# Two encoder layers on one core: the state-space tables' preparation on a new schedule, and the first q and k products begun on 256 tokens

## The chip, the core and the metric

The kernel runs on one NeuronCore of a Trainium2 chip. The time is the device time of one execution in microseconds (us). A core has TensorE (PE, with its weight loads shown as PEld), VectorE (DVE), ScalarE (ACT), GpSimd (POOL), and SyncE (SP), which here only issues DMAs. Each engine takes its own instructions strictly in the order in which they were written for it; a semaphore makes an instruction wait for another engine or for a DMA.

## The reference

Two layers over 1024 tokens of width 1024, each with a token mixer and a SwiGLU, both between RMSNorms. The first mixer is forgetting attention with 16 heads of 64, the second a state-space mixer (S5) with 64 groups of 16 channels and 64 states.

```python
for i in range(DEPTH):
    h = rmsnorm(x, mix_pre_gain[i])
    m = fox_mixer(h, ...) if i % 2 == 0 else s5_mixer(h, ...)
    x = x + rmsnorm(m, mix_post_gain[i])
    h = rmsnorm(x, ffn_pre_gain[i])
    x = x + rmsnorm((silu(h @ w_gate) * (h @ w_up)) @ w_down, ffn_post_gain[i])

# fox_mixer
proj = h @ w_in                       # q, k, v, gate, forget logits
q, k = rmsnorm(heads(q), q_gain), rmsnorm(heads(k), k_gain)
c = cumsum(log_sigmoid(f_logit + b_f))
s = q @ k.T * scale + c[q] - c[k]     # causal
o = softmax(s) @ v * sigmoid(gate);  return o @ w_out

# s5_mixer: x[t] = A x[t-1] + Bbar u[t];  y = Re(C x) + d * u
a = exp(lam * dt);  Bbar = (a - 1) / lam * B      # depends on the parameters alone
```

All of it is float32; a product is made of three float32r matmuls on high and low parts (high by high, high by low, low by high).

## The kernel before

**Order.** The code is written as generators that hand over to each other. A list scheduler then writes each engine's queue: it takes the instructions in the order of the code (some with a raised or lowered priority) and puts each where its own estimate of durations says that it is ready. On the chip the queues are followed as written, however long things really take.

**Start.** The 1024 tokens are eight blocks of 128. For each block `first_norm` squares the rows on ACT (L302), scales them on DVE (L325) or POOL (L318, L323), transposes them on PE in eight matmuls (L333) and splits the result into a high part (`hT`, cast on ACT, L335) and a low part (subtracted on DVE, L336). In the kernel before, four blocks are finished (`run(first_norm(range(0, 4), ...))`) and then the other four are woven with `qkv`, whose first work is the projection of q and of k for the first 512 tokens: 24 matmuls of 128x512 each, q's at L283, k's at L272 to L274. Their weights come as two DMAs of 512 KB (`raw`), are split on POOL (L253, L254), and are asked for behind the fourth and the sixth block of x. Behind that follow the forget logits (L392, L393) and q and k of tokens 512 to 1023 (L272 again).

**Gate and up of layer 0.** `gate_up` makes the gate and up products for 11 pairs of 128-column slices by a Strassen-like scheme: a pair is 14 steps of 12 matmuls of 128x512 (L853), each step into one of the bank pairs X, Y, Z of PSUM. X alternates between two bank pairs from one pair of slices to the next; Y is banks 4 and 5, Z banks 6 and 7. ACT and DVE split weights (L822, L823) and take results out of PSUM (L891 to L915).

**The tables.** Into these steps goes the preparation of the state-space tables, the generator `s5_params`: 27 pieces, one for each `next(beside, None)`, and a function `when(p, s)` says behind which step s of which pair p one is called. Pieces 1 to 8 are small DVE work (`s5_small`, L1028 to L1184), 9 and 10 transpose the C matrices (L1207, loaded by L1201), and pieces 11 to 27 make, for each of eight chunks of channels, two things in turn:

- odd piece: `finish` of the chunk before, which is eight transposes (L1223), one ACT copy into a page named `s5w1` (L1225) and its DMA to DRAM (`T_d`, L1226); then eight POOL operations (L1237, L1238, four L1241) that make `cp`. Their scratch `kg` is in the same page `s5w1`, so that they wait until that DMA has landed. ACT copies `bs` beside it (L1240).
- even piece: eight small products `pk` on PE (L1255) that read `cp`, their copies on ACT (L1258), and six POOL operations that make `bp` (L1298 to L1300), which the next odd piece transposes.

In the kernel before, the pieces stand at steps 8, 10, 12 of pair 0, at 5, 6, 8, 10, 12 of pair 1, at 5, 8, 12 of pair 2 and at 5 and 12 of every later pair. Their PSUM (`T.S`) is the bank pair Y (`T.slots = (4,)`).

The kernel's later stages (down projection, S5, the second layer's products) are not touched.

Of the kernel before, what the change touches and what calls it, by code (L numbers as in the profile page):

```python
# [10 lines left out]
F32R = mybir.dt.float32r  # L11
# [24 lines left out]
def f32(ap):  # L36
    return ap.bitcast(F32)
# [100 lines left out]
def weave(*streams):  # L138

    st = [[g, 0.0, max(t, 1e-6)] for g, t in streams]  # L140
    while st:
        s = min(st, key=lambda e: e[1] / e[2])
        try:
            s[1] += next(s[0])
        except StopIteration:
            st.remove(s)


def run(g):
    for _ in g:  # L150
        pass


def chain(*gs):
    for g in gs:
        yield from g


class Trunk:
# [113 lines left out]
        mm(ps, lh, rl, start=False, stop=False)  # L273
        mm(ps, ll, rh, start=False, stop=stop)  # L274

    def fm(self, ps, w, hT, half, step=4, apart=False):

        wh, wl = w
        h, l = hT[half]
        if apart:  # L280
            for n, (a, b) in enumerate(((wh, h), (wl, h), (wh, l))):
                for k in range(8):
                    self.nc.tensor.matmul(ps, a[:, k, :], b[:, k, :], start=n == k == 0, stop=n == 2 and k == 7)  # L283
                yield 0.65 * 8 / 3
            return
        for k in range(8):
            self.mm3(ps, wh[:, k, :], wl[:, k, :], h[:, k, :], l[:, k, :], k == 0, k == 7)
            if k % step == step - 1:
                yield 0.65 * step
# [118 lines left out]
        nc.vector.tensor_tensor_scan(z, ones, t1, 0.0, op0=ALU.mult, op1=ALU.add)  # L408
        nc.sync.dma_start(self.csum, z)

    def qk_proj(self, w, hT, hf, st, apart=False):
        nc = self.nc
        if "p" not in st:
            st["p"] = [self.R(f"p{i}", dt=F32R) for i in st["pages"]]
        ps = self.pb(self.proj)
        yield from self.fm(ps, w, hT, hf, apart=apart)
        X, Y = st[hf] = self.R("pt", (P, 2, 512)), self.R("pt", (P, 2, 512), F32R)
        with self.tc.high_priority(AHEAD):
            nc.scalar.copy(X[:, 1], ps)
            nc.vector.tensor_mul(X[:, 0], X[:, 1], X[:, 1])  # L420
        nc.scalar.copy(Y[:, 0], X[:, 0])
        nc.vector.tensor_sub(Y[:, 1], X[:, 0], f32(Y[:, 0]))
# [51 lines left out]
        tr(1)  # L474
        yield 0.5

    def qkv(self, hT, res, hp):


        v = []  # L480
        a, f, b = self.qkp if hp else ([9, 11, 8], [7, 35, 10], [12, 13, 14])
        q, k = dict(pages=a + f[2:]), dict(pages=f[:2])
        self.qkp = a[:2] + f[:1], b, [a[2], f[2], f[1]]
        if hp == 0:
            self.lsub, self.hcopy = self.nc.gpsimd, self.nc.gpsimd.tensor_copy
            wq, wk = self.take(), self.take(0)
            self.lsub, self.hcopy = self.nc.vector, self.nc.scalar.copy
            yield from self.qk_proj(wq, hT, 0, q, True)
            yield from self.qk_proj(wk, hT, 0, k)
            yield from self.forget_logits(hT)  # L490
            yield from self.qk_proj(wq, hT, 1, q)
            self.proj = (0, 1, 2, 3)
            with self.tc.issue_after(self.sqrt.ins):
                self.nc.scalar.preload_act_table_set(LNEXP)
            self.forget_sum()
            yield from self.qk_norm(0, 0, q)
            yield from self.qk_proj(wk, hT, 1, k)
            wv = self.take()
            yield from self.qk_norm(1, 0, k)
            yield from self.qk_norm(0, 1, q)  # L500
        else:
            wk = self.take()
            yield from self.qk_proj(wk, hT, 0, k)
            yield from self.qk_proj(wk, hT, 1, k)
            wq = self.take()
            yield from self.qk_norm(1, 0, k)
            yield from self.qk_proj(wq, hT, 0, q)
            yield from self.qk_norm(1, 1, k)
            yield from self.qk_proj(wq, hT, 1, q)
            wv = self.take()  # L510
            yield from self.qk_norm(0, 0, q)
        last = self.qk_norm(0, 1, q) if hp else self.qk_norm(1, 1, k)
        yield from self.v_proj(wv, hT, v, last)
        res.update(q=q["p"], k=k["p"], v=v)
# [132 lines left out]
    def fox(self, hT, og_d, begin, outr):  # L647
        c = [{} for _ in range(8)]
        o = [None] * 8
        weave((self.qkv(hT, c[0], 0), 11.0), (begin, 4.0))  # L650
        self.proj = PROJ
        self.R.set(pt=list(range(25, 29)))
        att = self.attend(c, o)
        held = [next(att)]

        def until(hp):
            while held and held[0][1] <= hp:
                yield held[0][0]
                held.clear()
                for x in att:  # L660
                    held.append(x)
                    break

        for hp in range(8):
            if hp == 7:
                a, f, b = self.qkp
                pages = f + [15, 16, 29, 33] + a + b + [17, 18, 19]
                self.R.set(woh=pages[0::2], wol=pages[1::2], **outr)
            fill = [self.pre_out(4)] if hp == 7 else [self.qkv(hT, c[hp + 1], hp + 1)]
            if hp:  # L670
                fill.insert(GP, self.gate(hp - 1, o, hT, og_d))
            weave((until(hp), 28.5 * AX), (chain(*fill), 34.0 * (hp < 7) + 10.4 * (hp > 0)))
        run(self.gate(7, o, hT, og_d))
# [125 lines left out]
    def gate_up(self, B, g_d, beside=iter(()), when=lambda p, s: False):  # L799
# [7 lines left out]
        nc, R = self.nc, self.R  # L807
        V = nc.vector
        n = NF // 2
# [64 lines left out]
        for p, s in order:  # L874
# [23 lines left out]
            a, b, x = steps[s // 2]  # L898
# [53 lines left out]
            if p == 0 and s > 11:  # L952
                prep[s - 10](1)
            if when(p, s):
                next(beside, None)
        yield

# [602 lines left out]
def trunk(ctx: ExitStack, tc: tile.TileContext, A, out):  # L1560
    T = Trunk(ctx, tc, A, out)
    nc, R = T.nc, T.R
    rg = lambda a, b: list(range(a, b))
    Wi = A["fox_w_in"][0]
    og_d = T.dram("og_d", [D, D])
# [31 lines left out]
    g_d = [[T.dram(f"g{i}{x}_d", [NF // 2, P, D if x < 3 else 512]) for x in range(4)] for i in range(2)]  # L1597
    T.ffn_plan(0, g_d[0], [T.rows(A["s5_w_in"][0], k * P, T.s5_w_in_cut(k)) for k in range(8)])
    for f in range(8):
        T.plan(T.cols(A["s5_w_glu"][0], f * P)[:3] + (("glu",) * 2 if f == 0 else (None,) * 2))  # L1600
        if f >= 1:
# [7 lines left out]
    OUT0 = dict(x=[23, 24], y=[25, 26, 27],  # L1609
                gn=[21, 22], ogk=[32])  # L1610
# [9 lines left out]
    hT = T.new_hT()  # L1620
    g0 = []

    def first_norm(tbs, banks):
        for tb in tbs:
            pool = tb in (5, 7)
            T.norm(xs[tb], g0[0] if pool else gps, ys[tb], pool, R("j") if pool else None)
            T.to_fm(ys[tb], T.hT_dst(hT, tb), banks)
            yield 1.0
# [10 lines left out]
    for tb in range(8):  # L1639
        xs[tb], ys[tb] = R("x"), R("y")  # L1640
        nc.sync.dma_start(xs[tb], x0[tb * P:tb * P + P, :])
        if tb == 3:
            T._load(0)
        if tb == 5:
            T._load(1)
            g0.append(T.gain("gn", A["mix_pre_gain"][0]))
    T.fox_setup()
    run(first_norm(range(0, 4), (0, 1, 2, 3)))
    T.fox(hT, og_d, first_norm(range(4, 8), (2, 3)), OUT0)
    xr = x0.rearrange("(p b) d -> p b d", b=8)  # L1650
    R.set(hold=[28, 30, 31, 34, 36, 37], t1=[20], ah=[3, 4, 20], al=[5, 6, 21], er=[29, 32])
    first = {0: (8, 10, 12), 1: (5, 6, 8, 10, 12), 2: (5, 8, 12)}
    B = Operands(T)
    gu = T.gate_up(B, g_d[0], T.s5_params(), lambda p, s: s in first.get(p, (5, 12)))
    end = T.out_proj(lambda tb: xr[:, tb, :], A["mix_post_gain"][0], A["ffn_pre_gain"][0], x1_d, turns, B, lambda: next(gu))
    orr = out[0].rearrange("(p b) d -> p b d", b=8)
    gp = []
# [12 lines left out]
        ys[tb] = m, T.rstd(m, R("fj"), out=T.rr5[:, tb:tb + 1])  # L1670

    R.set(ops=rg(7, 14) + [19] + rg(15, 19), a2=[36, 37], S=[23, 24], s=[26, 27, 25], up=[22, 35], gr=[7, 8], t1=[32], ez=[33], **EARLY)
    T.slots = (4,)
    gu.send(end)
    T.slots = (0, 2)
    R.set(t=[15, 16], gh=[9, 37, 3], gl=[10, 36, 18], wdh=[11, 12, 35, 28], wdl=[13, 5, 29, 32], m=rg(19, 27), s=[27], rx=[4], ry=[33, 34])
# [23 lines left out]
    B = Operands(T)  # L1700
    gu = T.gate_up(B, g_d[1])
# [60 lines left out]
```

## Time and profile before

| what | value |
|---|---|
| median of three runs (lowest, highest) | 2391.63 us (2391.47, 2392.79) |
| the profiled execution | 2391.49 us, of it 2389.4 us from first to last instruction |
| PE busy | 2342.8 us, 98% of the span |
| DVE, ACT, POOL busy | 1688.9, 1198.0, 446.8 us |
| PE on the chain that ended last | 80% of the span |
| mean granted TensorE clock | 0.997 |

"Busy" of PE counts a matmul from its start to its modelled end, and matmuls overlap; the pace of PE is therefore read from start to start. A row of the timeline gives start, duration, engine, line, operation, output and inputs, count, and in brackets the idle time before it and what ended it. A row of a table of windows gives, for each engine, busy time and number of instructions, then the granted clock, the share of the DMA engines and GB/s. Of the groups of `raw` and `g_d` transfers each moves 512 KB or 256 KB; the median from issue to landing is 4.3 us for a 512 KB weight load of gate.

### The profile page before, as it was taken

To read this page: it belongs to the slowest core of one execution; us is meant where nothing else is said; L and a number is where in the kernel's file an instruction comes from. 1 tells how busy PE (TensorE), PEld (TensorE's weight loads), DVE (VectorE), ACT (ScalarE), POOL (GpSimd) and SP (SyncE) were. 2 spreads that over 40 slices of the span, in tenths; PEclk is the share of its full clock that TensorE was granted. 3 is DMA by queue.
4 is the path that set the end of the run, shared out by engine and by line. 5 is a ranking of instruction groups with operands and counts; after the bars stand their busy time and mean duration, and the time that the engine had idled before them with its cause. 6 is when DMAs were issued, how large, how long until landed. Compare 5 with 4: busy or idle time off the path is not lost.

```text
span 2389.4 us, 31474 instructions
## 1 busy us (share of the span) xinstructions
PE 2342.8 (98%) x11687; PEld 1942.2 (81%) x11687; DVE 1688.9 (71%) x2687; ACT 1198.0 (50%) x2029; POOL 446.8 (19%) x425
## 2 busy tenths in 40 slices
PE   8999999999999999999999999999999999999997
PEld 6788888888788878888888889888888888888886
DVE  6867777678678966667768686853795655655867
ACT  6766676677745334434554662332463333333444
POOL 3222221223300034545620002410000000000003
PEclk9999999999999999999999999999999999999999
DMA  5121112211333444343598753543434323238874
GB/s 158 39 63 50 58 49 67 63 45 62 127 129 111 120 116 138 118 138 118 185 323 315 267 172 98 153 134 106 132 93 142 110 93 119 92 111 277 283 233 158
DMA packets 256587, 320.33 MB, mean 134 GB/s; under 512 B 34289, under 2 KB 184097, under 8 KB 256434
## 3 DMA queue, kind: packets, MB, share of 16 engines
q1 hardware_dynamic: 256434, 318.33, 41.6%
q8 instruction: 91, 1.49, 0.3%
q14 instruction: 62, 0.51, 0.1%
HBM read 240.56 MB, written 77.72 MB: 133 GB/s over the span
## 4 chain that ended last, share of the span: by engine, by line
PE 80%; DVE 10%; ACT 4%; issue 3%; DMA 1%; POOL 1%; SPq 0%; DVEq 0%; ACTq 0%; POOLq 0%
PE ps L853 32%; PE ps L974 16%; PE ps L272 7%; PE ps L273 7%; PE ps L274 7%; PE ps L615 2%; PE ps L596 2%; PE ps L558 1%; DVE ps L562 1%; PE ps L559 1%; DVE y L325 1%; ACT y L302 1%; DVE ptl L600 1%; POOL o L622 1%; PE ps L101 1%
## 5 line engine op out<-in xcount | busy, mean ns | idle before, releaser
L853 PE MATMUL ps<-B,ah 128*128 128x512 f32 x992 | 306.7, 390 | 0.8 <-DVE B L90 0.6
L974 PE MATMUL ps<-wdh,gl 128*128 128x512 f32 x616 | 240.1, 390 | 1.9 <-DVE gl L254 1.9
L974 PE MATMUL ps<-wdh,gh 128*128 128x512 f32 x616 | 240.6, 391 | 0.7 <-DVE s L895 0.6
L974 PE MATMUL ps<-wdl,gh 128*128 128x512 f32 x616 | 240.3, 390 | 0.8 <-DVE wdl L254 0.8
L853 PE MATMUL ps<-ops,ah 128*128 128x512 f32 x704 | 219.7, 393 | 2.1 <-ACT s L910 2.1
L853 PEld LDWEIGHTS ps<-B,ah 128*128 128x128 f32 x992 | 186.2, 188 | 40.7 <-DVE B L90 1.2
L272 PE MATMUL ps<-hT,wh 128*128 128x512 f32 x504 | 200.8, 398 | 1.1 <-DVE pt L436 0.6
L274 PE MATMUL ps<-hT,wl 128*128 128x512 f32 x504 | 198.5, 394 | 0.0
L273 PE MATMUL ps<-hT,wh 128*128 128x512 f32 x504 | 197.6, 392 | 0.0
L853 PE MATMUL ps<-B,al 128*128 128x512 f32 x496 | 193.2, 390 | 0.0
L253 ACT CAST gh<-gr 128x1024 fp32r<-128x1024 f32 (+1 forms) x78 | 81.1, 1039 | 163.3 <-PE ps L974 127.5
L853 PEld LDWEIGHTS ps<-ops,ah 128*128 128x128 f32 x704 | 132.2, 189 | 31.4 <-ACT s L910 2.6
L254 DVE TENSOR_TENSOR gl<-gr,gh 128x1024 fp32r<-128x1024 f32 (+1 forms) x78 | 98.0, 1258 | 79.7 <-ACT gh L253 79.5
L1713 POOL TENSOR_TENSOR y<-m,s 128x512 f32<-128x512 f32 x4 | 6.5, 1625 | 759.0 <-DMA raw<-in_ffn_w_down_dram 750.1
L823 DVE TENSOR_TENSOR al<-raw,ah 128x1024 fp32r<-128x1024 f32 x84 | 110.8, 1321 | 46.7 <-ACT ah L822 46.3
L553 POOL TENSOR_TENSOR An<-An,cmask 128x128 f32<-128x128 f32 x128 | 78.7, 616 | 341.7 <-DVE mx L562 309.9
L600 DVE TENSOR_TENSOR ptl<-ps,pth 128x512 fp32r<-128x512 f32 x192 | 102.4, 551 | 56.6 <-ACT pth L599 56.2
L853 PE MATMUL ps<-ops,al 128*128 128x512 f32 x352 | 137.8, 392 | 0.0
L974 PEld LDWEIGHTS ps<-wdh,gl 128*128 128x128 f32 x616 | 115.7, 188 | 26.8 <-DVE gl L254 2.7
L974 PEld LDWEIGHTS ps<-wdh,gh 128*128 128x128 f32 x616 | 115.7, 188 | 26.1 <-DVE s L895 1.3
L974 PEld LDWEIGHTS ps<-wdl,gh 128*128 128x128 f32 x616 | 115.7, 188 | 24.9 <-DVE wdl L254 1.5
L822 ACT CAST ah<-raw 128x1024 fp32r<-128x1024 f32 x84 | 88.3, 1052 | 90.3 <-PE ps L853 81.5
(379 smaller groups left out, 5913.4 us busy)
## 6 DMA issues: line engine op xcount, KB each, us to landing
raw<-in_ffn_w_down_dram SPq DMA_DIRECT2D x98, 512.0 KB, 5.2
gr<-g_d SPq DMA_DIRECT2D x76, 512.0 KB, 4.5
raw<-in_ffn_w_gate_dram SPq DMA_DIRECT2D x44, 512.0 KB, 4.3
raw<-in_ffn_w_up_dram SPq DMA_DIRECT2D x44, 512.0 KB, 4.2
g_d<-s SPq DMA_DIRECT2D x66, 256.0 KB, 2.2
raw<-in_fox_w_in_dram SPq DMA_DIRECT2D x32, 512.0 KB, 4.3
g_d<-up SPq DMA_DIRECT2D x44, 256.0 KB, 3.2
g_d<-up SPq DMA_DIRECT2D x21, 512.0 KB, 3.0
```

The source lines that it names most:

```text
L253: self.hcopy(h, src)
L254: self.lsub.tensor_sub(l, src, f32(h))
L272: mm(ps, lh, rh, start=start, stop=False)
L273: mm(ps, lh, rl, start=False, stop=False)
L274: mm(ps, ll, rh, start=False, stop=stop)
L553: nc.gpsimd.tensor_add(An[h][:, qs], An[h][:, qs], self.cmask)
L596: nc.tensor.transpose(p2[:, i], p[:, (g + i) * P:(g + i + 1) * P], self.ident)
L600: nc.vector.tensor_sub(dl, p2[:, 0:n], f32(dh))
L822: nc.scalar.copy(h, src)
L823: V.tensor_sub(l, src, f32(h))
L853: nc.tensor.matmul(bank, x[:, k], y, start=start and k == i == 0, stop=True, skip_group_check=True)
L974: nc.tensor.matmul(bank, x[:, j, t], y[:, j], start=start and i == 0, stop=True, skip_group_check=True)
```

## The change

Three edits.

1. Two blocks of 128 tokens are normalised instead of four before `qkv` begins, and `qk_first` makes q and k of tokens 0 to 511 in pieces of 256 tokens (`quarter`): q's and k's first 256 tokens, with one `next(begin)` (a further block) behind each, then the second 256 of both. The weight loads move up behind the second and the fourth block of x. The transposes go to PSUM banks 6, 7, 2 and 3 in turn.
2. The table's pieces get a list of steps for every pair. There are still 27. With the list, odd and even pieces of one chunk stand five steps apart in two chunks, six in four and eight in one; before they stood seven apart in all.
3. Their PSUM is the X bank pair that the running pair does not use.

```diff
+    def quarter(self, ps, w, hT, c):
+        wh, wl = w
+        h, l = hT[0]
+        s = slice(256 * c, 256 * c + 256)
+        for n, (a, b) in enumerate(((wh, h), (wl, h), (wh, l))):
+            for k in range(8):
+                self.nc.tensor.matmul(ps[:, s], a[:, k, :], b[:, k, s], start=n == k == 0, stop=n == 2 and k == 7)
+            yield 0.9
+
+    def qk_first(self, ws, hT, sts, begin):
...
+        for p, w in zip(ps, ws):
+            run(self.quarter(p, w, hT, 0))
+            next(begin)
+        for p, w, st in zip(ps, ws, sts):
+            yield from self.quarter(p, w, hT, 1)
+            self.qk_out(p, 0, st)
...
-            yield from self.qk_proj(wq, hT, 0, q, True)
-            yield from self.qk_proj(wk, hT, 0, k)
+            yield from self.qk_first((wq, wk), hT, (q, k), begin)
...
-        weave((self.qkv(hT, c[0], 0), 11.0), (begin, 4.0))
+        weave((self.qkv(hT, c[0], 0, begin), 9.0), (begin, 4.0))
...
             if when(p, s):
+                self.slots = (p % 2 * 2 ^ 2 ^ self.X0,)
                 next(beside, None)
...
+        if tb == 1:
+            T._load(0)
         if tb == 3:
-            T._load(0)
+            T._load(1)
         if tb == 5:
-            T._load(1)
...
-    run(first_norm(range(0, 4), (0, 1, 2, 3)))
-    T.fox(hT, og_d, first_norm(range(4, 8), (2, 3)), OUT0)
+    run(first_norm(range(0, 2), (2, 3, -2, -1)))
+    T.fox(hT, og_d, first_norm(range(2, 8), (2, 3, -2, -1)), OUT0)
...
-    first = {0: (8, 10, 12), 1: (5, 6, 8, 10, 12), 2: (5, 8, 12)}
+    table = {0: (9, 12), 1: (6, 9, 12), 2: (4, 8, 12), 3: (2, 5, 9), 4: (2, 7, 12), 5: (5, 11), 6: (3, 9), 7: (2, 7, 12),
+             8: (4, 10), 9: (2, 8), 10: (2, 8)}
...
-    gu = T.gate_up(B, g_d[0], T.s5_params(), lambda p, s: s in first.get(p, (5, 12)))
+    gu = T.gate_up(B, g_d[0], T.s5_params(), lambda p, s: s in table[p])
...
-    T.slots = (4,)
```

What this does to the queues is shown at three places. First PE at the start of the program, before: `y` are the normalised blocks that are transposed, `hT` their high and low parts, `wh` and `wl` the split weights of q.

```order
L333 MATMUL ps<-ident,y_110 128x128 x8
L333 MATMUL ps<-ident,y_113 128x128 x8
L333 MATMUL ps<-ident,y_116 128x128 x8
L333 MATMUL ps<-ident,y_119 128x128 x8
L283 MATMUL ps<-hT_99,wh_269 128x512 x8
```

The same place after (the transposes are now L327, and the products of 256 tokens L412):

```order
L327 MATMUL ps<-ident,y_110 128x128 x8
L327 MATMUL ps<-ident,y_113 128x128 x8
L412 MATMUL ps<-hT_99,wh_221 128x256 x8
L412 MATMUL ps<-hT_99,wl_222 128x256 x8
L412 MATMUL ps<-hT_100,wh_221 128x256 x8
L412 MATMUL ps<-hT_99,wh_227 128x256 x5
L327 MATMUL ps<-ident,y_118 128x128 x8
L412 MATMUL ps<-hT_99,wh_227 128x256 x3
```

The products of q and of k now stand behind the second block, and the third block's transposes behind 29 of them.

Next ACT in the second half of pair 2 (no. 2), before: `s_7713` and `up_7714` are the pair's results out of PSUM, `R` the page that holds `bs`, `bb` a result of the small DVE work.

```order
L908 COPY s_7713<-ps 128x512
L1240 COPY R_775_7414<-bb_7612 64x4x16 x2
L908 COPY up_7714<-ps 128x512
L1240 COPY R_775_7414<-bb_7612 64x4x16 x2
L822 CAST ah_7773<-raw_7479 128x1024
L910 COPY s_7713<-ps 128x512
```

The same place after:

```order
L926 COPY s_7707<-ps 128x512
L926 COPY up_7708<-ps 128x512
L840 CAST ah_7775<-raw_7478 128x1024
L928 COPY s_7707<-ps 128x512
L840 CAST ah_7799<-raw_7725 128x1024
L928 COPY up_7708<-ps 128x512
L1259 COPY R_782_7533<-bb_7910 64x4x16 x4
```

The copies of `bb` moved from between the results of steps 4, 5 and 6 to behind that of step 7.

Last ACT between the copy of an odd piece's transposes (`s5w<-ps 128x1024`) and the copies of the even piece behind it (`s5w<-ps 16x4x128`), before; the rows between are weight splits and results of the steps, and `S` and `raw` are weights.

```order
L1225 COPY s5w_847_8196<-ps 128x1024
L822 CAST a_867_8391<-raw_8097 128x512
L903 COPY s_8233<-ps 128x512
L903 COPY up_8234<-ps 128x512
L822 CAST ah_8278<-S_8275 128x1024
L891 ACTIVATE s_8233<-s_8233 128x512
L822 CAST ah_8298<-raw_8021 128x1024
L908 COPY s_8302<-ps 128x512
L908 COPY up_8303<-ps 128x512
L1240 COPY R_775_7414<-bb_7612 64x4x16
L1258 COPY s5w_862_8346<-ps 16x4x128 x2
```

The same chunk after (the pieces stand at steps 7 and 12 of pair 4):

```order
L1244 COPY s5w_866_8409<-ps 128x1024
L909 ACTIVATE s_8323<-s_8323 128x512
L840 CAST ah_8470<-raw_8393 128x1024
L909 ACTIVATE s_8232<-s_8232 128x512
L840 CAST ah_8496<-S_8493 128x1024
L909 ACTIVATE s_8323<-ps 128x512
L840 CAST a_886_8637<-raw_8343 128x512
L1277 COPY s5w_874_8522<-ps 16x4x128 x2
```

Eight rows of the steps' work and a copy of `bs` stood between the two, now six rows. On PE, 84 matmuls of 128x512 stood between the transposes and the `pk` products of every chunk; now 60, 72, 72, 60, 72, 72 and 96 for the chunks 1 to 7, counted in the two queues.

More of the change, by code (lines that the diff above doesn't have):

```diff
@@ L274, in mm3, with fm @@
         mm(ps, ll, rh, start=False, stop=stop)
-    def fm(self, ps, w, hT, half, step=4, apart=False):
+    def fm(self, ps, w, hT, half, step=4):
         wh, wl = w
         h, l = hT[half]
[L280 to L285, printed above, removed]
         for k in range(8):
@@ L409, in forget_sum, with qk_proj @@
         nc.sync.dma_start(self.csum, z)
-    def qk_proj(self, w, hT, hf, st, apart=False):
-        nc = self.nc
+    def quarter(self, ps, w, hT, c):
[7 more added lines that the diff above has]
+    def qk_first(self, ws, hT, sts, begin):
+        for st in sts:
+            st["p"] = [self.R(f"p{i}", dt=F32R) for i in st["pages"]]
+        ps = [self.pb(self.proj) for _ in ws]
+        for p, w in zip(ps, ws):
[4 more added lines that the diff above has]
+            self.qk_out(p, 0, st)
+    def qk_proj(self, w, hT, hf, st):
         if "p" not in st:
@@ L415, in qk_proj, with qk_out @@
         ps = self.pb(self.proj)
-        yield from self.fm(ps, w, hT, hf, apart=apart)
+        yield from self.fm(ps, w, hT, hf)
+        self.qk_out(ps, hf, st)
+    def qk_out(self, ps, hf, st):
+        nc = self.nc
         X, Y = st[hf] = self.R("pt", (P, 2, 512)), self.R("pt", (P, 2, 512), F32R)
@@ L475, in v_proj, with qkv @@
         yield 0.5
-    def qkv(self, hT, res, hp):
+    def qkv(self, hT, res, hp, begin=None):
         v = []
```

## The prediction

> **What bounds the kernel.** I read the page's shares first, then windows, then PE's waits, and last the timelines of all engines where PE waits.
>
> ```profile
> PE 2342.8 (98%) x11687; PEld 1942.2 (81%) x11687; DVE 1688.9 (71%) x2687; ACT 1198.0 (50%) x2029; POOL 446.8 (19%) x425
> 760.00:900.00 140.00, 135.01 (x603) 110.34 (x602) 114.58 (x236) 53.48 (x86) 21.27 (x16) 0.98 0.42 114
> 900.00:1100.00 200.00, 200.00 (x957) 164.36 (x956) 137.85 (x148) 80.83 (x125) 106.52 (x80) 1.00 0.40 127
> 859.04 5.60 PE L853 MATMUL ps<-ops,a 128*128 128x512 f32 x24
> 864.48 0.62 PE L853 MATMUL ps<-B,ah 128*128 128x512 f32 x2
> ```
>
> PE is busy 98% of the span. In gate and up it loses 5 us between 760 and 900 and nothing from 900 to 1100, so every wait that the change takes from PE or gives to PE counts in full. The pace is (864.48 - 859.04) / 24 = 0.2267 us for a 128x512 matmul; a step of 12 is 2.72 us.
>
> **Part 1, the start.**
>
> ```profile
> 8.74 3.89 PE L333 MATMUL ps<-ident,y 128*128 128x128 f32 x16 [2.65 <-DVE rr L309]
> 15.83 3.78 PE L333 MATMUL ps<-ident,y 128*128 128x128 f32 x16 [3.19 <-DVE y L325]
> 19.48 2.31 PE L283 MATMUL ps<-hT,wh 128*128 128x512 f32 x8
> 29.84 1.03 PE L333 MATMUL ps<-ident,y 128*128 128x128 f32 x8
> 30.64 0.48 PE L272 MATMUL ps<-hT,wh 128*128 128x512 f32 x1
> 34.25 1.87 PE L393 MATMUL ps<-hT,wf 128*48 128x512 f32 x7
> 41.71 0.39 PE L272 MATMUL ps<-hT,wh 128*128 128x512 f32 x1
> 12.44 1.06 ACT L335 CAST hT<-ps 128x512 fp32r<-128x512 f32 x2
> 8.11 1.06 ACT L302 ACTIVATE y<-x 128x1024 f32<-128x1024 f32 x1 [0.28 <-DMA x<-in_x_dram]
> 11.22 1.04 POOL L253 CAST wh<-raw 128x1024 fp32r<-128x1024 f32 x1 [8.55 <-DMA raw<-in_fox_w_in_dram]
> 79.64 0.28 PE L558 MATMUL ps<-p,p 128*128 128x256 f32 x1
> 79.88 0.40 PE L274 MATMUL ps<-hT,wl 128*128 128x512 f32 x1
> ```
>
> Now PE waits 3.19 us for block 2, and q's first product starts at 19.48; the first product of q's second 512 tokens starts at 41.71. With the change q needs only the casts of block 1, the first of which ends at about 13.0. Its weights come third in the queue, where the third block of x landed at 8.1 (ACT squares it then); with POOL's 1.04 us cast they are there long before. The third block lands one transfer later, hidden, because ACT now squares it behind the casts of block 0. From 13.0 PE has: 96 products of 256 tokens at 0.12 (two of that width take 79.64 to 79.88) = 11.5; six blocks of transposes at 0.80 (29.84 to 30.64) = 4.8; the forget logits, 34.25 to 41.71, = 7.5; one product of the q norm, 0.2. That is 24.0, and 37.0 without losses. Losses: at the start the clock is half (16 transposes take 3.78 us at 15.83, eight take 0.80 later). I take it as half until about 16.6, one stretch of PE work of the length that ran slow before: 3.6 us at half rate loses 1.8. The products behind the transposes of blocks 3 and 7 wait for a cast each, 0.7 in all. So 39.5 against 41.71: -2.2 us. If the clock rises at once, -4.0; if only at 19.98 as late as before, -0.5. The PSUM banks and the earlier weight loads I cost at nothing; the covers are the waits named.
>
> **Part 2, the waits of pair 2.**
>
> ```profile
> 831.92 0.50 PE L853 MATMUL ps<-T,al 128*128 128x512 f32 x1 [1.36 <-DVE al L823]
> 842.06 0.82 PE L853 MATMUL ps<-ops,ah 128*128 128x512 f32 x2 [2.14 <-ACT s L910]
> 844.80 1.94 PE L1207 MATMUL ps<-ident,s5w 128*128 128x128 f32 x8 [1.49 <-DMA s5w<-in_s_c_re_dram]
> 839.96 0.49 ACT L1240 COPY R<-bb 64x64 f32<-64x64 f32 x2 [2.08 <-DVE bb L1184]
> 829.78 0.95 DVE L1153 TENSOR_SCALAR s5t<-R 128x448 f32<-128x448 f32 x1
> 842.60:849.40 6.80, 5.31 (x17) 4.05 (x16) 3.94 (x5) 2.44 (x4) 0.00 (x0) 0.50 0.98 183
> 849.40:856.20 6.80, 6.80 (x35) 5.67 (x35) 3.19 (x4) 1.79 (x3) 4.39 (x4) 1.00 0.02 5
> ```
>
> These are the 5 us: 1.36 for a weight split that stands in DVE's queue behind the small table work, 2.14 because ACT stands at a copy of `bb` that DVE has not made, 1.49 for the C matrices, whose load waited for the same DVE work. After them the granted clock is 0.50 for 6.8 us; the 5.31 us of PE work there take twice their time, 2.65 lost. Together 7.64.
>
> The list puts pieces 4 to 8 later (step 9 of pair 1 to step 12 of pair 2, before step 5 to 12 of pair 1) and the copies of `bb` behind step 7's result. So the 2.14 should go, the 1.49 too (the C transposes now come four steps, 10.9 us, behind their loads), and the clock stays up. The DVE work itself is only moved: I leave one wait like the 1.36, with bounds 0 and 3.5 (1.36 + 2.14). Part 2: -7.64 + 1.4 = -6.2.
>
> **Part 3, the chunks.** An odd piece's transposes start a chain that an even piece's products wait for.
>
> ```profile
> 901.05 1.03 PE L1223 MATMUL ps<-ident,s5w 128*128 128x128 f32 x8
> 917.38 3.33 POOL L1241 TENSOR_TENSOR s5w<-s5w 64x512 f32<-64x512 f32 x2
> 921.07 1.05 PE L1255 MATMUL ps<-s5w,R 128*16 128x128 f32 x16
> 1021.59 1.03 PE L1223 MATMUL ps<-ident,s5w 128*128 128x128 f32 x8
> 1022.85 1.03 ACT L1225 COPY s5w<-ps 128x1024 f32<-128x1024 f32 x1
> 1023.92 0.38 SPq L1226 DMA_DIRECT2D T_d<-s5w  x1
> 1027.68 1.10 POOL L1237 TENSOR_TENSOR s5w<-cc,pw 128x512 f32<-128x512 f32 x1 [12.18 <-DMA T_d<-s5w]
> 1035.22 3.85 POOL L1241 TENSOR_TENSOR s5w<-s5w 64x512 f32<-64x512 f32 x2
> 1041.61 0.62 PE L1255 MATMUL ps<-s5w,R 128*16 128x128 f32 x8
> 1052.01 3.43 POOL L1300 TENSOR_TENSOR s5w<-s5w,s5w 128x512 f32<-128x512 f32 x2
> 1061.77 1.03 PE L1223 MATMUL ps<-ident,s5w 128*128 128x128 f32 x8
> 1078.63 3.31 POOL L1241 TENSOR_TENSOR s5w<-s5w 64x512 f32<-64x512 f32 x2
>   POOL s5w L1241: 0.4, 1
> ```
>
> Transposes, copy, a DMA of 3.8 us, then 11.4 us of POOL: from 1021.59 to 1035.22 + 3.85 = 1039.07, 17.5 us, the shortest of the seven chunks. From 901.05 it is 19.7, from 1061.77 it is 20.2, the longest. Seven steps of PE work between, 901.05 to 921.07, are 20.0, so before only once a product waits for POOL, 0.4 us (last row, from the view of L1255). The chain does not get shorter by the change: same operations, same page, same DMA.
>
> PE's work between transposes and products is now 0.79 + 60 x 0.2267 = 14.4 us in two chunks and 0.79 + 72 x 0.2267 = 17.1 in four; with 96 it is 22.6, no wait. PE is in order, so whatever the chain lacks is idle: at 17.5 us 3.1 and 0.4 a chunk, at 20.2 us 5.8 and 3.1. I take the middle, 18.8: 2 x 4.4 + 4 x 1.7 = 15.6 us, bounds 7.8 and 24. Behind the waiting product stand all the pair's matmuls; ACT and DVE starve with it. The way back, product to `bp` to the next transposes, takes 1052.01 + 3.43 - 1041.61 (the chunk's products, 20.02 behind its transposes) = 13.8; five steps and the products are 14.6, so I cost it at nothing (up to 1 us where ACT is late). The X banks are free from the last read of the pair before to the next pair's first step, and the copies of about 1 us fit into the 2.7 of a step: nothing.
>
> A wait of 4.4 us is as long as the 2.14 and 1.49 together behind which the clock was halved. I take one of the two long ones to halve it: 2.65, bounds 0 and 5.3. The Trainium skill ("TensorE: Matmul & The Clock Gate", "Why this matters for your kernels") would have the clock kept unless PE idles for about 3 us. Here it fell after 2.14, so the measurement decides that shorter waits suffice. By that rule both waits of 4.4 us would halve it, and the sum would be 2.65 higher.
>
> **Sum.** -2.2 - 7.6 + 1.4 + 15.6 + 2.65 = +9.8. The profiled execution is 2391.49 (span 2389.4 and 2.1 around it), 0.14 under the median, so 2401.3.
>
> **Rivals.**
> Both long waits halve the clock: for it speaks that only one matmul of 0.1 us stands inside each; against it, that between 900 and 1100 nothing of the kind can be seen. 2401.3 + 2.65 = 2404.
> The gains and waits cancel: the chain stays near its shortest, 17.5 us (7.8 in all), no clock is lost: -2.2 - 7.6 + 1.4 + 7.8 = -0.6, 2390.9. For it: DVE has less to do at the chunks' side when PE stands, and POOL's pair L1241 takes 3.31 in one chunk and 3.85 in another, so POOL's time varies. Against it: two of three chunks shown take over 19.
> Faster: the chain shrinks with PE's pause to 16 us, for instance by a T_d transfer that finds the DMA engines free. Then only the two short distances wait, 2 x 1.6 = 3.2, and with no DVE wait left the sum is -2.2 - 7.6 + 3.2 = -6.6, 2384.9. It decides below about 16.3 us; no chunk comes near.
> The first pieces do not start earlier, because the clock stays half and casts are late: +2.2, 2403.5. Against it: the cast at 12.44 and PE's 3.19 us wait.
>
> **Chances.** Forecast 0.42, both clocks 0.24, cancel 0.21, faster 0.09, no early start 0.04. A difference of 0.2% (4.8 us) is about what can be told from none: slower 0.70, same 0.21, faster 0.09. From all bounds the ends are 2391.5 - 4.0 - 7.6 + 7.8 = 2387.7 and 2391.5 - 0.5 - 7.6 + 3.5 + 24 + 5.3 = 2416. Without the outer tenth on each side: 2390 to 2411.
>
> **What would show it.** In the profile after: q's first product near 13 us and the second 512 tokens near 39.5; between 820 and 850 no wait for ACT's `s` or the C load, the clock 1.0; the products at L1274 waiting for POOL L1260 in pairs 4 and 7 for over 3 us each and in four others for 0.4 to 3; PE busy under 195 of 200 us between 900 and 1100. It is wrong if those products start without a wait, if POOL's chain from transposes to `cp` is under 16.5 us, or if waits of pair 2 come back elsewhere.

## The result: 1.4% slower, more than three times the loss that was forecast

| kernel | median of the runs, us | ratio to before (95% interval) |
|---|---|---|
| before | 2392.21 | 1 |
| changed | 2426.35 (2426.13 to 2428.61) | 1.0143 (1.0131 to 1.0155) |

The profiled execution of the changed kernel has a span of 2424.4 us, 35.0 more than before. First the two windows of the prediction, and two rows of PE's timeline at the start:

```profile
760.00:900.00 140.00, 133.08 (x582) 108.84 (x581) 104.73 (x227) 47.95 (x74) 12.54 (x8) 0.98 0.41 112
900.00:1100.00 200.00, 183.32 (x852) 147.70 (x853) 130.02 (x138) 73.12 (x116) 104.64 (x78) 0.96 0.37 118
13.00 1.79 PE L412 MATMUL ps<-hT,wh 128*128 128x256 f32 x8 [0.34 <-ACT hT L329]
38.91 0.39 PE L272 MATMUL ps<-hT,wh 128*128 128x512 f32 x1
```

The start did what the prediction said: the first q product is at 13.00, the second 512 tokens at 38.91, 2.8 us earlier than before. At the first step of gate and up (738.06 before, 735.86 after) 2.2 of them are left. Then PE, which never paused between 900 and 1100, is idle for 16.7 of 200 us, at a granted clock of 0.96. PE's waits from gate and up of layer 0 to the first step behind it (engine, what waits, for whom: us in total, times, longest):

```profile
PE ps L1274 <- POOL s5w L1260: 18.5, 10, 5.8
PE ps L871 <- DVE al L841: 8.2, 5, 3.3
PE ps L871 <- DVE up L930: 1.8, 1, 1.8
PE ps L993 <- DVE s L913: 1.6, 1, 1.6
PE ps L871 <- ACT ah L840: 0.4, 1, 0.4
```

At the end of the stage the changed kernel is 32.4 us behind (1218.33 against 1185.93 for the last step). The terms against before:

| term | us |
|---|---|
| start, as it arrives at gate and up | -2.2 |
| pair 2: 5.1 of waits and 3.0 of the clock, before 5.0 and 2.65 | +0.5 |
| products waiting for POOL's `cp` | +18.5 |
| clock halved in pairs 4 (3.3), 7 (1.9) and 9 (1.7) | +6.9 |
| other waits of PE, from pair 3 on: `al` 3.0, `up` 1.8, `ah` 0.4 | +5.2 |
| sum | +28.9 |

For a stretch at half clock the loss is half of PE's busy time in it. Of the 3.5 us that are missing, 2.0 are the first matmuls behind a wait: measured from start to start, the ten waits of the first row cost 20.5 and not 18.5. The weight loads of the transposes wait 0.7 in two places; about 1 us stays open. Another 2.9 us come between this stage and layer 1's gate and up: the row for `s` above stands at the first step of the down projection (0.6 before), and a wait of 1.3 us there for DVE's `m` (L1017) is new.

**One chunk, followed back.** The longest wait is that of chunk 4, in pair 7. Rows of the timelines of PE, SP, DVE, ACT and POOL, and one of SP's waits:

```profile
1046.48 0.71 PE L1242 MATMUL ps<-ident,s5w 128*128 128x128 f32 x5
SPq L950 <- DVE up L947: 8.7, 1, 8.7
1041.88 1.77 DVE L947 TENSOR_TENSOR up<-s 128x512 f32<-128x512 f32 x1
1047.36 0.39 SPq L231 DMA_DIRECT2D raw<-in_ffn_w_gate_dram  x1
1051.38 0.69 DVE L853 TENSOR_TENSOR S<-raw 128x512 f32<-128x512 f32 x1 [4.46 <-DMA raw<-in_ffn_w_gate_dram]
1052.70 0.64 ACT L909 ACTIVATE s<-s 128x512 f32<-128x512 f32 x1 [4.53 <-DVE s L923]
1053.24 0.99 ACT L1244 COPY s5w<-ps 128x1024 f32<-128x1024 f32 x1
1057.01 1.11 POOL L1256 TENSOR_TENSOR s5w<-cc,pw 128x512 f32<-128x512 f32 x1 [13.05 <-DMA T_d<-s5w]
1065.52 3.79 POOL L1260 TENSOR_TENSOR s5w<-s5w 64x512 f32<-64x512 f32 x2
1067.69 0.61 PE L1274 MATMUL ps<-s5w,R 128*16 128x128 f32 x2 [5.81 <-POOL s5w L1260]
```

The transposes start at 1046.48. Their ACT copy stands behind a silu, the silu behind DVE's `s`, DVE behind `S`, which waits for a gate load, and that load was issued only at 1047.36, because four stores of `s` and `up` stood before it on SP, each of which waited for DVE: 8.7 us at the first, which went out at 1043.68, then 0.5, 0.7 and 0.8. So the copy comes at 1053.24 instead of a microsecond behind the transposes, and the chain to `cp` takes 22.8 us where the prediction had 18.8. The other six chunks took 21.3, 18.8, 20.0, 19.2, 18.4 and 18.6.

**The clock's falls.** Windows of 3.41 us (PE's busy time is the first number behind the comma, the granted clock the third from the end):

```profile
939.37:942.78 3.41, 1.09 (x5) 0.56 (x3) 3.41 (x4) 1.10 (x2) 3.33 (x3) 1.00 0.00 0
942.78:946.20 3.42, 0.61 (x2) 0.13 (x2) 3.39 (x3) 0.00 (x0) 3.27 (x3) 0.50 0.00 0
946.20:949.61 3.41, 2.63 (x16) 1.78 (x17) 2.48 (x3) 0.57 (x1) 0.72 (x1) 0.50 0.56 222
949.61:953.02 3.41, 3.41 (x9) 2.65 (x9) 0.00 (x0) 1.45 (x5) 2.57 (x3) 0.50 0.22 85
1147.58:1151.00 3.42, 1.34 (x7) 0.92 (x6) 3.39 (x5) 2.21 (x6) 0.45 (x1) 1.00 0.21 50
1151.00:1154.41 3.41, 3.41 (x10) 2.67 (x9) 2.09 (x3) 2.55 (x5) 1.38 (x1) 0.50 0.34 101
```

In this profile all the starts of half clock in gate and up (843.80, 942.78, 1065.66, 1151.00) lie whole multiples of 3.413 us apart. Each follows a window in which PE idled for over 2 us. A wait of 2.08 us that falls into one window is enough (pair 9); the 1.3 and 0.9 us in pair 6, split over two windows, are not.

### The profile page after: what moved, and what is told of

Same layout as the page of the kernel before. It is cut to its first block, busy times and chain, and to the rows that moved or that the text cites. A ratio compares the mean times of both kernels' runs of the same rounds, so it can differ in the third digit from the quotient of the medians.

```text
span 2424.4 us, 31574 instructions
## 1 busy us (share of the span) xinstructions
PE 2353.4 (97%) x11735; PEld 1946.7 (80%) x11735; DVE 1697.8 (70%) x2687; ACT 1195.7 (49%) x2029; POOL 454.0 (19%) x425
## 4 chain that ended last, share of the span: by engine, by line
PE 68%; DVE 14%; DMA 5%; ACT 5%; POOL 4%; issue 4%; SPq 0%; DVEq 0%; ACTq 0%; POOLq 0%
PE ps L871 24%; PE ps L993 13%; PE ps L272 7%; PE ps L273 6%; PE ps L274 6%; PE ps L633 2%; PE ps L614 2%; POOL s5w L1260 2%; DVE al L841 1%; DMA raw<-in_ffn_w_gate_dram 1%; PE ps L576 1%; DMA raw<-in_ffn_w_up_dram 1%; DVE ps L580 1%; DMA raw<-in_ffn_w_down_dram 1%; PE ps L577 1%
## 5 line engine op out<-in xcount | busy, mean ns | idle before, releaser
L272 PE MATMUL ps<-hT,wh 128*128 128x512 f32 x496 | 197.2, 398 | 0.7 <-DVE pt L455 0.2
L273 PE MATMUL ps<-hT,wh 128*128 128x512 f32 x496 | 194.3, 392 | 0.0
```

The costliest lines, as they stand in the source:

```text
L272: mm(ps, lh, rh, start=start, stop=False)
```

## The experiments

### Each edit alone

The first edit alone, with before's steps and banks:

```diff
-    table = {0: (9, 12), 1: (6, 9, 12), 2: (4, 8, 12), ...}
+    first = {0: (8, 10, 12), 1: (5, 6, 8, 10, 12), 2: (5, 8, 12)}
...
-                self.slots = (p % 2 * 2 ^ 2 ^ self.X0,)
...
+    T.slots = (4,)
     gu.send(end)
```

> Only the first edit (two blocks first, q and k begun on 256 tokens); the table's steps and its banks are those of before. Theory A, each edit costs for itself: in the changed kernel the second 512 tokens began 2.8 us earlier and gate and up 2.2 us earlier, so 2392.2 - 2.2 to 2.8, about 2389.7, and pair 2's waits are those of before (1.4, 2.1, 1.5, clock 0.50 once). Rival B, the early start is given back in attention or by other loads: 2392, within 0.5.

Measured: 2390.27 us, ratio 0.9989 (0.9981 to 0.9998). Theory A: the start is worth its 2 to 3 us, by itself (the interval leaves 0.5 to 4.5).

The second and third edits alone, with before's start:

> Only the second and third edits (the new steps, the X banks); the start is that of before. Theory A: all of the loss is here, 2426.35 + 2.2 to 2.8, about 2429; products behind cp wait for POOL 18 to 20 us in all, weight splits of DVE about 8 us, the granted clock falls four times in gate and up. Rival B, the loss comes from the two edits meeting (transfers of the start shifted against the table): clearly under 2426, near 2400 as I had forecast.

Measured: 2434.05 us, ratio 1.0174 (1.0160 to 1.0188); waits for POOL 21.0 us, for `al` 10.9. All of the loss is here. It is 7.7 us more than the changed kernel has, where the start accounts for 2 to 3; in its profile the clock is halved for 30.7 us of gate and up, in the changed kernel's for 27.3, and once more near 2408.

The third edit alone:

> Only the third edit (the table's PSUM in the X banks of the other parity), with before's start and steps. Theory A, banks cost nothing: 2392, within 1. Rival B, the pieces wait for the X banks or their copies hold X up: over 2395, with waits of transposes or of first steps of a pair on ACT copies.

Measured: 2394.28 us, ratio 1.0005 (0.9996 to 1.0014). The banks cost nothing that can be told, and PE has the same three waits in gate and up (2.1, 1.6, 1.6 us).

### Is it the copy's page that makes the chain long?

The first try gave the copy of the transposes page 14:

```diff
+        if "s5T" not in R.r:
             R.widen("raw", 14)
...
-            T = R("s5w1", (P, D))
+            T = R("s5T", (P, D))
...
+    R.set(s5T=[14])
     gu.send(end)
```

> The changed kernel, but the copy of the transposes that goes to DRAM has a page of its own (page 14, which the weights give up: three weight pages instead of four in this stage), so that POOL's scratch kg need not wait for the copy and its DMA. Theory A, that copy and landing are the part of the chain that makes the products wait: the chain is 0.8 for the transposes and POOL's 11.8 to 13.8, 14.6 at most against 14.4 to 17.1 of PE work, so the waits for POOL fall from 18.5 to under 2 us, two or three of the clock's falls go, pair 2's waits stay: 2426.35 - 17 - 5 = about 2404, between 2400 and 2408. Rival B, POOL is slow for another reason: over 2420. Rival C, the missing weight page makes PE wait for weights: waits for raw DMAs, over 2410.

Measured: 2425.44 us, ratio 1.0140 (1.0127 to 1.0154). The expectation described this edit wrongly: gate and up begins, and takes page 14 for weights, before the line that sets the new ring, so weights and copies shared the page. PE's longest waits in gate and up:

```profile
PE ps L871 <- ACT s5T L1245: 15.0, 3, 8.6
PE ps L871 <- DVE al L841: 5.6, 3, 3.3
PE ps L1275 <- ACT s5T L1245: 4.4, 1, 4.4
```

No product waits for POOL any more, as the theory's first half has it; but PE now stands still elsewhere, which gives POOL time, so this run alone does not settle it. ACT's copy waits for the weight splits that read page 14, and holds PSUM and all of ACT's queue: 19.4 us.

The second try put the copy where nobody else works:

```diff
-            T = R("s5w1", (P, D))
-            nc.scalar.copy(T, ps.rearrange("p a b c -> p (a b c)"))
-            nc.sync.dma_start(self.T_d[ch], T)
+            f = ps.rearrange("p a b c -> p (a b c)")
+            for a, b, T in ((0, 512, self.R2[:, 0:512]), (512, 896, self.pwt[:, 576:960]),
+                            (896, 1024, self.R2[:, 768:896])):
+                nc.scalar.copy(T, f[:, a:b])
+                nc.sync.dma_start(self.T_d[ch][:, a:b], T)
```

> The changed kernel, but the copy of the transposes that goes to DRAM lies in three pieces (512, 384 and 128 columns) in free columns of the pages R2 and pw, shared with no weights and not with POOL's scratch kg; three ACT copies and three DMAs instead of one each. Theory A, the products wait because kg waits for that copy and its DMA: kg can start when bp is done, the chain behind the transposes is POOL's 11.8 to 13.8 alone, under the 14.4 of PE work; the waits for POOL (18.5 us in all) go, the three falls of the clock in pairs 4, 7 and 9 go (6.9), and of the waits for weight splits and results of DVE from pair 3 on (some 5 us) most, since they follow PE's stops; pair 2's 5.1 us and its clock stay: 2426 - 18.5 - 6.9 - 3 = about 2397, between 2393 and 2403. Rival B, POOL's own time is too long for the list: 2415 and over, waits for cp stay over 10 us. Rival C, the three small copies hold ACT up: waits for ACT, over 2405.

Measured: 2403.64 us (2400.38 to 2405.47), ratio 1.0044 (1.0029 to 1.0060), 22.7 us less than the changed kernel. PE's waits in gate and up, and the window of the prediction:

```profile
PE ps L871 <- DVE al L841: 8.7, 5, 3.3
PE ps L871 <- DVE up L930: 2.3, 1, 2.3
PE ps L1244 <- POOL s5w L1322: 1.3, 1, 1.3
900.00:1100.00 200.00, 194.84 (x926) 157.90 (x925) 151.70 (x143) 79.36 (x138) 119.08 (x86) 0.98 0.39 124
```

No product waits for `cp` any more, with the same list of steps. The copy and its DMA in POOL's page were the wait. The median lies just outside my range's upper end, because the waits for `al` and `up` did not shrink with it (3.8 and 2.3 us from pair 3 on) and two of them, of 2.3 us each, halved the clock for one window behind them.

### Do seven steps cure it?

```diff
-    table = {..., 4: (2, 7, 12), 5: (5, 11), 6: (3, 9), 7: (2, 7, 12), 8: (4, 10), 9: (2, 8), 10: (2, 8)}
+    table = {..., 4: (2, 7), 5: (0, 5, 12), 6: (3, 10), 7: (1, 8, 13), 8: (6, 11), 9: (4, 9), 10: (2, 7)}
```

> The changed kernel with another list for the chunks: the products stand seven steps behind their transposes in every chunk (84 matmuls), the next transposes five steps behind those (60). Pieces 1 to 11 as in the change. Theory A, the steps between transposes and products set the wait: in the changed kernel the chain from transposes to cp took 18.4 to 22.8 us, seven steps are 19.8, so the products' waits for POOL fall from 18.5 us to under 4 and two of the clock's falls go with them. But five steps (14.6 us with the products) are less than products to bp there (14.6 to 19.2), so the transposes wait in their turn, 4 to 12 us in all: 2405 to 2416. Rival B, the way back doesn't bind: no waits of transposes, 2400 to 2404. Rival C, the waits come from POOL's total work, not from the steps: 2426.

Measured: 2425.46 us, ratio 1.0136 (1.0120 to 1.0151). PE's waits from pair 3 on:

```profile
PE ps L1242 <- POOL s5w L1319: 9.5, 8, 1.9
PE ps L993 <- DVE s L913: 3.4, 1, 3.4
PE ps L871 <- ACT ah L840: 3.0, 1, 3.0
PE ps L1274 <- POOL s5w L1260: 2.2, 4, 1.0
PE ps L871 <- ACT up L928: 2.1, 1, 2.1
```

The products' waits fell from 18.5 to 2.2, as theory A has it, and the transposes wait 9.5 instead. The time did not fall. The rest is in the rows for `s`, `ah` and ACT's `up`, 8.5 us where the changed kernel has 2.0 (the waits for `al` fell, from 3.0 to 0.4), and in the clock, which fell five times from pair 3 on, each time for a window in which PE was busy throughout (8.5 us lost, 6.9 in the changed kernel). Why just these three waits grew was not tried. I missed the total by 10 us. A likely reason, not tried, is the list as a whole: it starts the chunks at step 9 of pair 3 and leaves twelve steps for each, where before started at step 12 of pair 2 and left fourteen.

### Pair 2

Pieces 1 to 8 back at their old steps, the rest as changed:

```diff
-    table = {0: (9, 12), 1: (6, 9, 12), 2: (4, 8, 12), 3: (2, 5, 9), ...}
+    table = {0: (8, 10, 12), 1: (5, 6, 8, 10, 12), 2: (), 3: (2, 5, 9), ...}
```

> The changed kernel, but pieces 1 to 8 (the small DVE work) at their steps of before, none in pair 2; pieces 9 to 27 stay where the change put them. Theory A, the 1.9 and 3.3 us for weight splits in pair 2 and the halved clock behind them come from table work that stands ahead of the splits in DVE's queue: one wait of about 1.4 stays, no clock loss in pair 2, so 2426.35 - 6.7 = about 2419.6; the waits for POOL in the chunks stay at 18 to 20 us. Rival B, the splits are late for another reason (the X banks, ACT): no change, 2426. A chunk's wait that falls otherwise on the clock can move it by 2 to 3.

Measured: 2422.90 us, ratio 1.0121 (1.0105 to 1.0136): 3.5 us less, half of what I expected. ACT's timeline says why:

```profile
834.63 0.50 ACT L1259 COPY R<-bb 64x64 f32<-64x64 f32 x2 [4.90 <-DVE bb L1200]
837.70 0.50 ACT L1259 COPY R<-bb 64x64 f32<-64x64 f32 x2 [2.08 <-DVE bb L1203]
```

These copies of `bb` belong to a piece that the code calls at step 9 of pair 3. The scheduler put them into pair 2, as soon as it thinks `bb` is ready, and so ACT stands there as before (PE: 2.1 us for `s`, 1.0 for `al`). In the changed kernel it was DVE alone; DVE's rows and PE's:

```profile
842.92 0.59 DVE L1176 TENSOR_SCALAR R<-R 128x448 f32<-128x448 f32 x1
843.41 1.22 DVE L841 TENSOR_TENSOR al<-raw,ah 128x1024 fp32r<-128x1024 f32 x1
844.69 0.79 PE L871 MATMUL ps<-ops,al 128*128 128x512 f32 x1 [3.26 <-DVE al L841]
```

Six table operations over 448 columns, from 838.14 on and among them one of the steps' own, stand ahead of the split that PE waits for. With the small pieces at their old steps the same six run from 826.09 to 834.01, mixed with more of the steps' work, and one wait of 1.0 us for a split is left.

The last try (e8_best in a later expectation) joins the first edit with three cures for pair 2: small pieces earlier, C transposes later, and chunk 0's copies of `bb` on POOL, which had nothing to do there.

```diff
-                    nc.scalar.copy(self.bs[half[i], :, gi], self.bb[half[gi], i, pr])
+                    (nc.scalar.copy if ch else G.tensor_copy)(self.bs[half[i], :, gi], self.bb[half[gi], i, pr])
...
-    first = {0: (8, 10, 12), 1: (5, 6, 8, 10, 12), 2: (5, 8, 12)}
+    first = {0: (6, 9, 11), 1: (4, 5, 7, 9, 11), 2: (9, 11, 13)}
```

> The first edit alone, with before's steps from pair 3 on and Y banks, and three things for pair 2: the small pieces a little earlier (steps 6, 9, 11 of pair 0, 4, 5, 7, 9, 11 of pair 1), the C transposes and the first cp later (9, 11, 13 of pair 2), and the first chunk's copies of bb on POOL, so that ACT doesn't stand at them. Theory A, pair 2's loss is DVE's queue, ACT at bb and the late C loads, and the clock that falls behind them: 1.4 + 2.1 + 1.6 and 1.7 to 2.7 of the clock go, 2390.3 - 7 = 2383. Rival B, the DVE work collides with pair 0 or 1 instead: 2387 to 2391. Rival C, the later C transposes make the first chunk late: new waits for POOL in pairs 3 and 4, over 2388.

Measured: 2385.55 us (2384.71 to 2389.77), ratio 0.9971 (0.9962 to 0.9980): faster than both kernels. A window over pair 2, PE's one wait in pairs 1 and 2, and ACT's row there:

```profile
820.00:860.00 40.00, 40.00 (x187) 33.29 (x186) 34.35 (x48) 15.59 (x22) 10.96 (x8) 1.00 0.45 117
PE ps L871 <- ACT s L928: 1.9, 1, 1.9
799.93 0.23 ACT L1127 ACTIVATE s5t<-s5t 128x32 f32<-128x32 f32 x1 [2.69 <-DVE s5t L1126]
```

PE has no gap in the 40 us and the clock stays. One new wait stands in pair 1, where ACT now comes to the table's sine before DVE has its argument; with the clock's fall behind it (1.7 us) it is 3.6 of the 5.5 us by which this profiled run, 2388.54 us, misses the 2383 expected; the median misses it by 2.5.

### Is it idle time that lowers the clock?

```diff
+            if ch in (1, 4):
+                for i in range(10):
+                    nc.tensor.matmul(pk.rearrange("p q n -> p (q n)"), self.ident,
+                                     self.bb[:, 0].rearrange("p a c -> p (a c)"), start=True, stop=True)
```

> The changed kernel with ten extra matmuls of 128x512 (identity by bb, overwritten afterwards) ahead of the products of chunks 1 and 4, where PE waited 4.8 and 5.8 us; at 0.10 us per 128 columns of such a float32 matmul I take 0.4 each, 4 us. The output is the same. Theory A, the clock falls because PE idles: with the gap filled it stays at 1.00 in pairs 4 and 7 and the products start when they did, so 3.3 and 1.9 us are saved: 2421. Rival B, the clock falls for another reason than the idle time: it falls again, 2426. Rival C, the extra matmuls delay the products: over 2427.

Measured: 2425.55 us, ratio 1.0140 (1.0126 to 1.0154). Around the two gaps in this kernel:

```profile
939.70:950.00 10.30, 10.30 (x42) 5.21 (x41) 7.49 (x7) 1.87 (x5) 6.88 (x6) 1.00 0.36 127
1060.00:1070.00 10.00, 10.00 (x39) 4.65 (x38) 7.62 (x5) 1.74 (x4) 6.95 (x4) 1.00 0.20 59
```

And in the changed one:

```profile
940.00:950.00 10.00, 4.09 (x22) 2.24 (x21) 8.64 (x8) 2.06 (x4) 6.97 (x6) 0.64 0.23 91
1061.00:1071.00 10.00, 3.12 (x20) 1.56 (x19) 8.82 (x5) 1.53 (x2) 8.08 (x5) 0.73 0.09 32
```

With PE kept busy the clock stays at 1.00 in both places, while POOL and DVE do what they did: the idle time lowers it. Ten of these matmuls took 8.7 us, not 4 (each is two passes of 0.43), which still ends about where PE's wait did: the steps go on at 948.50, in the changed kernel at 948.79. Yet the total did not move. From the first step of gate and up to its last, the profiled run gains 2.9 us on the changed kernel's, though three short waits there now fall badly on the grid (half clock at 832, 1024 and 1191); two more behind the stage (1577, 2403) spend the gain. The four runs spread from 2421.94 to 2428.24, and the profiled one is the slowest, so the total neither shows the gain nor rules it out.

The start was the last place to try:

```diff
+    fill = T.bank(4, 1, (P, 512))
+    for i in range(2):
+        nc.tensor.matmul(fill, ones, grow[:, 0:512], start=True, stop=True)
```

> The kernel e8_best with two more matmuls of the gain row (1x512, two passes each, as the two there; their result is not used) at the start, behind those two, where PE idled 2.7 us before the first transposes. Theory A, the clock is decided on a grid of 3.41 us: a stretch of the grid in which PE idles over about 1.8 us is followed by one at half clock, and from half clock it comes back only behind a stretch with under about 0.6 us idle; so PE busy from 2.3 us on brings the full clock by 9.1 us at the latest instead of 14 to 20: the 16 transposes take 1.6 us instead of 3.9, the first products start near 12 instead of 13 and run at full rate: 2385.5 - 2 to 3 = 2383. Rival B, the clock rises at a fixed time after the start: no change, 2385.5. Rival C, the extra matmuls delay the transposes and nothing is gained: 2386 to 2388.

Measured: 2388.01 us, ratio 0.9978 (0.9969 to 0.9987). This is the median of eleven runs, of which one took 9023.70 us; the other ten lie between 2386.22 and 2391.93, with a median of 2387.63, 2.1 us more than without the two matmuls. The two intervals overlap, so a loss is not shown, but no gain is there.

```profile
5.78 3.62 PE L1659 MATMUL ps<-grow,ones 1*128 1x512 f32 x4
9.33 3.67 PE L327 MATMUL ps<-ident,y 128*128 128x128 f32 x16
13.59 2.05 PE L412 MATMUL ps<-hT,wh 128*128 128x256 f32 x8 [0.58 <-ACT hT L329]
14.37:17.79 3.42, 3.42 (x18) 3.42 (x18) 3.26 (x11) 2.43 (x6) 2.99 (x2) 1.00 1.03 408
17.79:21.20 3.41, 3.41 (x31) 3.41 (x31) 1.81 (x3) 1.59 (x3) 1.76 (x1) 1.00 0.75 152
```

PE was busy from 2.2 to 13.0 us, and still ran at half rate until 17.79: 18 matmuls in the window before, 31 in the one behind (the granted clock in the rows says 1.00 there, so at the start the rate must be read from the count). Theory A is wrong for this stretch. The rise lies on the grid of this run's later falls, behind a window full of products. The transposes started at 9.33 instead of 8.53 and the first product at 13.59 instead of 12.76, as rival C has it. Matmuls over one row, which filled the window of 4.14 to 7.55, did not bring the rise, nor did the window of 10.96 to 14.37, with 2.0 us of transposes, 0.6 idle and 0.8 of products; in the changed kernel 1.7, 0.3 and 1.4 were enough, at 14.36.

The Trainium skill says ("TensorE: Matmul & The Clock Gate", Part 4) that transposes do not count as busy in the same way. Here they did count where they filled a window: with the third edit alone, with the copy in page 14 and with the copy in free columns, the rise came behind a window with 3.3 to 3.4 us of transposes and no product (at 12.58, 12.42 and 11.85). The last of these, where the first eight products, which took 2.05 us above, take 1.19:

```profile
8.56 3.65 PE L327 MATMUL ps<-ident,y 128*128 128x128 f32 x16 [2.41 <-DVE rr L303]
12.79 1.19 PE L412 MATMUL ps<-hT,wh 128*128 128x256 f32 x8 [0.58 <-ACT hT L329]
```

Behind windows with about 0.35 us idle and 2.2 to 2.9 of transposes (the first edit alone, the ten extra matmuls, e8_best) it did not come. So of the two kinds it is the matmuls over one row that did not bring the full clock by themselves.

## Why the prediction was wrong

The sign was right, the size was not: +34 us against +10, and outside the range.

1. **Start, -2.2.** Right: -2.8 at the second 512 tokens, -2.2 at gate and up, -2.3 in the total of the first edit alone. The first product came at 13.00, as worked out. The clock rose at 14.36 instead of 16.6, worth 1.1 us, which small losses took up in part, so the closeness is partly luck. The rise moves from run to run (11.85 to 17.34 in eight profiles with the new start), and gate and up with it: it begins at 734.89 to 736.95 in those eight, and at 738.06 to 739.65 in the three with the old start.
2. **Pair 2, -6.2: wrong, +0.5.** The step that failed is "The DVE work itself is only moved: I leave one wait like the 1.36". Two waits came, 1.87 and 3.26 us, and the clock fell again (3.0). The bound of 3.5 was set by waits of before; it should have been worked out from DVE's queue. The two causes that I named, ACT's copy of `bb` and the C load, did go, and DVE's queue took their place.
3. **Chain, 18.8 us: a little short.** It measured 19.9 on average, 18.4 to 22.8. "The chain does not get shorter" was right, that it gets no longer was assumed: in chunk 4 a store on SP waited for DVE, a load stood behind it, DVE waited for that load and ACT's copy for DVE. POOL's part also grew, from 11.4 to 12.1 us to 11.8 to 13.8. Term by term: 15.6 forecast, 18.5 measured (20.5 from start to start), inside its bounds.
4. **Clock, 2.65: mis-sized, 6.9 from pair 3 on.** The price of one fall was right (1.7 to 3.3), their number was not: three, not one. What decides is idle time within a window, not the wait's length, so that a wait of 2.1 us was enough in pair 9.
5. **No further waits: wrong, +5.2, and 2.3 behind the stage.** "ACT and DVE starve with it" stood in the text without a term. PE waited for `al`, `up` and `ah` in pairs 3, 7, 9 and 10. With the products' waits gone (the copy in free columns) 3.8 us of `al` and 2.3 of `up` remained, so they don't need PE's stops. With before's list (the first edit alone) PE has no wait at all between pair 2 and the end of the stage, so they come with the new list; which of DVE's operations make them was not followed.
6. **The way back, nothing.** Right for this list, where the transposes' weight loads waited 0.7 us in all, and wrong as a rule: with five steps everywhere it cost 9.5.

All four misses have one sign: 6.7 us in pair 2, 4.9 in the chain (from start to start), 4.2 in the clock, and 5.2 and 2.9 without a term make 23.9 of the 25.2 us between the 35.0 measured and the 9.8 forecast. The terms were taken one by one, each at the middle of its bounds, though the queues of SP, DVE, ACT and POOL hang on one another.

## What to carry to other kernels

Before moving work in a static schedule, follow each chain to its shared buffer: here the whole wait was one page that a copy and its DMA held while another engine wanted it as scratch, and free columns elsewhere took out all 18.5 us of it. A chain that runs in a loop through three engines needs its full period: lengthening one leg at the cost of the other moved the wait from products to transposes and won nothing. And where an in-order engine is already full for tens of microseconds, moving work inside that stretch moves the wait with it; look for an engine that is idle there.

## What the runs showed of the hardware

**The clock is decided on a grid of 3.41 us whose phase differs from run to run.** In each of the twelve profiles all falls behind the start lie on one grid, with another offset in each. Over these profiles all 50 windows with more than 1.90 us of PE idle were followed by half clock, of the 40 with 1.49 to 1.90 eleven were, and below that none. From half clock, again behind the start, windows with 0.72 us of idle or more stayed there, and those with 0.57 or less came back; of two between, one stayed (0.61) and one came back (0.62). The same wait of 2.6 us near 1541 us shows it: in before's profile it is split, 0.75 and 1.80 us in two windows, and costs nothing; in the first edit's profile 2.0 of it lie in one. Before:

```profile
1538.91:1542.32 3.41, 2.66 (x36) 2.29 (x33) 3.40 (x8) 1.17 (x3) 3.00 (x2) 1.00 0.61 176
1542.32:1545.73 3.41, 1.61 (x14) 1.61 (x15) 3.41 (x5) 0.00 (x0) 3.26 (x3) 1.00 0.48 105
```

The first edit alone:

```profile
1538.87:1542.28 3.41, 1.40 (x13) 1.13 (x10) 3.40 (x8) 1.07 (x2) 3.28 (x3) 1.00 0.48 146
1542.28:1545.69 3.41, 2.85 (x13) 2.85 (x14) 3.41 (x6) 0.00 (x0) 2.12 (x2) 0.50 0.70 208
```

That would account for the scatter of one kernel's runs (before: 2389.5 to 2395.2 in 21 runs), and by my estimate from these numbers a change that removes one wait of 2 us is worth 2 to 4 us on the mean: the wait, and in a part of the runs a fall that costs 1.7 us or more. A free-running window of this length is what the Trainium skill describes ("TensorE: Matmul & The Clock Gate", Part 1); these runs agree on its length, and show that a window need not be idle throughout: more than 1.9 us of 3.41 sufficed each time.

**DVE and POOL are slower beside each other.** In gate and up of before the weight split `al` (128x1024) takes 1.22 us where POOL is idle (37 of them, the median) and 1.76 where POOL works nearly throughout (15). POOL's products into `kg` average 1.14 us where DVE works during at most nine tenths of their time (22 of the 32 of before) and 1.75 where it works for more of it (10); over all 32 the mean is 1.33 us in before and 1.49 in the changed kernel. DVE worked during 60% of the time of these products and the operations that make `cp` from them in before, and 76% in the changed kernel. This fits the growth of POOL's part of the chain, which the prediction took as fixed.
